# NSA attention in a two-layer decoder trunk: value products with the split values as weights, and the NSA norm moved behind the output projection

## The chip, the cores and the metric

One NeuronCore of a Trainium2 chip runs the whole program. The time is device microseconds (us) of one execution; the runs given below are separate executions of the same program. Engines: PE (TensorE, matrix products and transposes), DVE (VectorE), ACT (ScalarE), POOL (GpSimd), SP (SyncE, which issues most of the DMAs).

## The reference

Two layers, each of four parts on 512 tokens of 1024 features: a half-step FFN, a hybrid token mixer, cross-attention to 256 memory tokens, and another half-step FFN. The change is in the mixer:

```python
o_nsa = nsa_mixer(q_n, kc, vc, ks, vs, kw, vw, gates, ...)   # 8 heads of 64
o_nsa = rms_norm(o_nsa, nsa_out_g)                            # over its 512 features
o_ret = retention(q_r, k_r, v_r, g_r, ret_gn_g)               # 4 heads of 128
return jnp.concatenate([o_nsa, o_ret], axis=-1) @ w_out
```

`nsa_mixer` sums three branches for each head, weighted by gates: attention over 31 compressed blocks, over selected blocks and over a window. With 512 tokens the selected and the window branch both see every key up to the query, so both are plain causal attention with an ALiBi slope, with keys and values of their own. `retention` multiplies the scores by a decay instead of a softmax and normalises each head.

## The kernel before

Activations stand feature-major in eight [128 features x 512 tokens] chunks. Most products are made of two float32r parts for each operand (`unit` L82 and `split` L122 make a high part on ACT, whi or oh, and the rest on DVE, wlo or ol); `mm3` (L116) then issues three float32r matmuls (L117 to L119). Products with small or few operands are in plain fp32.

`mixer` (L398) runs once per layer. It computes the compressed branch (`cmp_attn`), then 16 head-branches, 8 heads by 2 branches. For one branch `head_scores` (L589) makes, for each of the four query blocks, two score matmuls (keys as high and low part, ps_s, 512, 384, 256 and 256 columns), a DVE operation that adds ALiBi and takes the extreme of the row (L610), and the exponential on ACT with its sum (L612). `head_out` (L615) makes ten transposes of p (ps_pt), copies them to SBUF (pT, ACT or DVE), ten fp32 products with the block of pT as the stationary and 64 columns of values as the moving operand (L634, ps_po), scales by gate over sum on DVE (L640) and adds to onsa [tokens x features] on POOL (L642). `head_out` of a branch is written behind `head_scores` of the next.

Then come the inputs of retention: qr and kr (`fm_plain`, ps_fm) and vr and gr (`tm`, token-major, ps_tm); the norm of onsa (L673 to L681); `ret_scores` (L693: ps_rs, times decay on DVE, ra); `to_fm` (L684), which transposes onsa and splits it (ps_ot, oh, ol); `ret_out` (L705: ps_ro, normalisation and gate on DVE, oret); `to_fm` for oret; `out_proj` (L215), eight output chunks of 24 matmuls each (ps_o); and `postnorm`.

The order on each engine is set when the program is built, by a scheduler that draws independent work forward; each engine then runs its list in order and waits where an operand is not there. PSUM has eight tiles of a bank: four for the accumulators of the projections (`acc`: ps_fm, ps_tm, ps_o) and four for the rest (`aux`: ps_s, ps_pt, ps_po, ps_rs, ps_ro, ps_ot). SBUF tiles come from pools with a fixed number of buffers. So ps_fm, ps_tm and ps_o matmuls stand as filler between the steps of the heads and of retention, as far as accumulators allow.

## Time and profile before

| | |
|---|---|
| median of 3 runs | 2512.14 us (2511.12 to 2512.42) |
| span of the profiled execution | 2510.8 us |
| PE busy | 2447.7 us, 97% |
| DVE busy | 1389.5 us, 55% |
| ACT busy | 902.0 us, 36% |
| POOL busy | 260.9 us, 10% |
| mixer of layer 0, first score of the first branch | 508.2 us |
| first score of the 16th branch | 625.8 us |
| end of the last ps_o matmul | 721.5 us |

The busy shares are means over the whole span; the windows of the mixer show them stage by stage. PE's matmuls are pipelined and a record's duration contains the drain, so the price of one matmul is read from the distance between starts. The granted clock (PEclk) is a share of full speed, 2.4 GHz; the lower level is 1.2 GHz.

### The profile page before, as it was taken

The page shows a single profiled execution, that of the slowest core. Times are in us where ns is not written, and L with a number is a line of the kernel's source. Part 1 is how long each engine was busy: PE and PEld are TensorE (multiplying, and loading weights), DVE is VectorE, ACT ScalarE, POOL GpSimd, SP SyncE. Part 2 cuts the span into 40 slices and gives each one's busy share as a digit, 9 for nine tenths or more (in the row PEclk, how much of TensorE's full clock was granted, in tenths as well). Part 3 has the DMA queues.
Part 4 walks back from the last instruction along what each step waited for, and adds up shares of the span by engine and source line. Part 5 has one row for each costly group of instructions (what it writes and reads, how often), then busy time and mean ns, then how long its engine had stood idle before and what let it go on. Part 6 is the DMA issues. An engine that isn't in the chain of part 4 may idle for free.

```text
span 2510.8 us, 31031 instructions
## 1 busy us (share of the span) xinstructions
PE 2447.7 (97%) x12184; PEld 2039.7 (81%) x12184; DVE 1389.5 (55%) x2518; ACT 902.0 (36%) x1480; POOL 260.9 (10%) x218
## 2 busy tenths in 40 slices
PE   8999999999999999999999999999999998999997
PEld 6888878888877878888878888878888777888887
DVE  6434458465776574344474344574657765634454
ACT  4322243255344442322342222332553543322222
POOL 0000023001040120000120000130010402100002
PEclk9999999999999999999999999999999999999999
DMA  4323343411232233233323232324112322232321
GB/s 170 100 98 95 98 121 109 145 43 35 76 109 85 93 101 95 98 93 100 111 101 96 97 93 101 109 93 144 43 34 70 101 68 67 86 100 92 102 94 58
DMA packets 74594, 233.64 MB, mean 93 GB/s; under 512 B 8272, under 2 KB 17744, under 8 KB 74448
## 3 DMA queue, kind: packets, MB, share of 16 engines
q1 hardware_dynamic: 65232, 222.21, 27.8%
q10 hardware_dynamic: 9216, 9.44, 1.3%
q8 instruction: 96, 1.57, 0.3%
q14 instruction: 50, 0.41, 0.1%
HBM read 229.53 MB, written 2.10 MB: 92 GB/s over the span
## 4 chain that ended last, share of the span: by engine, by line
PE 89%; DVE 7%; ACT 2%; DMA 1%; issue 1%; POOL 0%; SPq 0%; POOLq 0%; ACTq 0%; DVEq 0%
PE ps_gu L118 12%; PE ps_gu L117 12%; PE ps_gu L119 12%; PE ps_dn L118 6%; PE ps_dn L119 6%; PE ps_dn L117 6%; PE ps_po L634 3%; PE ps_o L118 2%; PE ps_o L119 2%; PE ps_o L117 2%; DVE xsl L184 2%; PE ps_fm L118 2%; PE ps_fm L119 2%; PE ps_fm L117 2%; PE ps_tm L118 1%; PE ps_tm L119 1%
## 5 line engine op out<-in xcount | busy, mean ns | idle before, releaser
L88 ACT ACTIVATE whi<-raw 128x1024 fp32r<-128x1024 f32 (+2 forms) x402 | 417.8, 1040 | 1104.2 <-PE ps_gu L118 331.5
L89 DVE TENSOR_TENSOR wlo<-raw,whi 128x1024 fp32r<-128x1024 f32 (+2 forms) x402 | 491.6, 1223 | 295.6 <-ACT whi L88 289.1
L117 PE MATMUL ps_gu<-xsh,whi 128*128 128x512 f32 (+1 forms) x1424 | 552.0, 389 | 11.9 <-ACT whi L88 9.0
L118 PE MATMUL ps_gu<-xsl,whi 128*128 128x512 f32 (+1 forms) x1424 | 554.8, 390 | 7.8 <-DVE xsl L184 7.4
L119 PE MATMUL ps_gu<-xsh,wlo 128*128 128x512 f32 (+1 forms) x1424 | 552.3, 388 | 0.8 <-DVE wlo L89 0.7
L118 PEld LDWEIGHTS ps_gu<-xsl,whi 128*128 128x128 f32 x1424 | 268.6, 189 | 70.0 <-DVE xsl L184 16.3
L117 PEld LDWEIGHTS ps_gu<-xsh,whi 128*128 128x128 f32 x1424 | 268.7, 189 | 66.4 <-ACT whi L88 9.0
L119 PEld LDWEIGHTS ps_gu<-xsh,wlo 128*128 128x128 f32 x1424 | 268.6, 189 | 55.4 <-DVE wlo L89 1.9
L157 POOL TENSOR_TENSOR ssq<-ssq,sq 128x512 f32<-128x512 f32 (+1 forms) x84 | 131.9, 1571 | 1714.3 <-ACT sq L156 1711.3
L118 PE MATMUL ps_dn<-hl,whi 128*128 128x512 f32 (+1 forms) x704 | 268.4, 381 | 2.2 <-DVE hl L126 2.2
L117 PE MATMUL ps_dn<-hh,whi 128*128 128x512 f32 (+1 forms) x704 | 268.2, 381 | 0.0
L119 PE MATMUL ps_dn<-hh,wlo 128*128 128x512 f32 (+1 forms) x704 | 268.0, 381 | 0.0
L278 DVE TENSOR_TENSOR u<-ps_gu,rstd_bc 128x512 f32<-128x512 f32 x88 | 60.8, 691 | 217.8 <-PE ps_gu L119 217.8
L274 DVE TENSOR_TENSOR g<-ps_gu,rstd_bc 128x512 f32<-128x512 f32 x88 | 60.8, 691 | 184.0 <-PE ps_gu L119 181.2
L118 PEld LDWEIGHTS ps_dn<-hl,whi 128*128 128x128 f32 x704 | 132.3, 188 | 28.9 <-DVE hl L126 3.4
L117 PEld LDWEIGHTS ps_dn<-hh,whi 128*128 128x128 f32 x704 | 132.3, 188 | 25.6
L119 PEld LDWEIGHTS ps_dn<-hh,wlo 128*128 128x128 f32 x704 | 132.3, 188 | 25.0
L301 DVE TENSOR_TENSOR y<-ps_dn,y 128x512 f32<-128x512 f32 x56 | 38.7, 691 | 131.6 <-PE ps_dn L119 131.6
L118 PE MATMUL ps_fm<-xsl,whi 128*128 128x512 f32 x256 | 104.6, 409 | 3.4 <-DVE xsl L184 3.3
L117 PE MATMUL ps_fm<-xsh,whi 128*128 128x512 f32 x256 | 103.3, 405 | 0.0
L119 PE MATMUL ps_fm<-xsh,wlo 128*128 128x512 f32 x256 | 102.2, 400 | 1.0 <-DVE wlo L89 1.0
L612 ACT ACTIVATE p<-p,smx 128x512 f32<-128x512 f32 (+3 forms) x128 | 70.4, 552 | 87.2 <-DVE smx L610 87.0
(226 smaller groups left out, 3749.7 us busy)
## 6 DMA issues: line engine op xcount, KB each, us to landing
raw<-in_ffn_gu_dram SPq DMA_DIRECT2D x176, 512.0 KB, 3.3
raw<-in_ffn_dn_dram SPq DMA_DIRECT2D x64, 448.0 KB, 3.3
raw<-in_ffn_dn_dram SPq DMA_DIRECT2D x32, 512.0 KB, 3.5
raw<-in_win_fm_dram SPq DMA_DIRECT2D x32, 512.0 KB, 3.3
raw<-in_wk_dram SPq DMA_DIRECT2D x16, 512.0 KB, 3.5
raw<-in_cmp_w_dram SPq DMA_DIRECT2D x16, 512.0 KB, 3.7
raw<-in_wout_dram SPq DMA_DIRECT2D x16, 512.0 KB, 3.5
raw<-in_wv_dram SPq DMA_DIRECT2D x16, 512.0 KB, 3.5
```

The costliest lines, as they stand in the source:

```text
L88: act.activation(hi, raw, AF.Copy)
L89: dve.tensor_tensor(lo, raw, hi.bitcast(F32), op=ALU.subtract)
L117: pe.matmul(ps, ah, bh, start=start, stop=False)
L118: pe.matmul(ps, ah, bl, start=False, stop=False)
L119: pe.matmul(ps, al, bh, start=False, stop=stop)
L157: eng.tensor_tensor(acc_t, acc_t, sq, op=ALU.add)
L184: dve.scalar_tensor_tensor(lo, x[c][:, ts_], g, hi.bitcast(F32), op0=ALU.mult, op1=ALU.subtract)
L274: dve.tensor_tensor(g1, pss[0], bc, op=ALU.mult)
L278: dve.tensor_tensor(u1, pss[1], bc, op=ALU.mult)
L301: dve.tensor_tensor(y[c], ps, y[c], op=ALU.add)
L612: act.activation(pr[i], pr[i], AF.Exp, bias=m, scale=-1.0, accum_out=sums[:, i : i + 1])
L634: pe.matmul(po[:, i], blk[i, j], vsel[j // 2][:, j % 2, col : col + DH], start=j == 0, stop=j == i)
```

## The change

The value products change sides: the values of a key block, split into high and low part side by side (vsel, 128 columns of weights), are the stationary operand, and the transposed probabilities, split too (pTh on ACT, pTl on DVE), move. For key block j all queries from block j on move at once: 512, 384, 256 and 128 columns, in float32r, each twice (high and low). Both branches of a head accumulate into one ps_po tile, whose lower and upper 64 rows are the products with the two parts of the values; ACT copies one half, DVE adds the other, POOL adds to onsa, which is now feature-major [128 x 512] in four chunks. Since the result is feature-major, the gate over the sum can't be applied to it per row; p itself is multiplied by it on DVE, before the transposes. The compressed branch is normalised ahead of its transposes too, and its products become feature-major.

The transposes of onsa fall away: each chunk is gained and split as it is. Its norm is a factor per token, and that is applied behind the projection: `out_mixed` computes the NSA half of an output chunk, multiplies it by the row nsa_bc (1/rms, broadcast by PE) and adds the retention half, accumulated in a bank of its own. The squares of onsa are summed on ACT, POOL and DVE. In `down_halves` the fourth chunk's weights are held in buffers of another pool.

```diff
...
             y.append(yc)
         return y, ssq
+    def out_mixed(src, l, parts, bc):
+        (h1, l1), (h2, l2) = parts
+        y, ssq = [], None
+        w = {}
+        def half(c, oh, ol, k0):
+            wh, wl = w[c]
+            ps = acc("ps_o")
+            for k in range(4):
+                s = slice((k0 + k) * P, (k0 + k + 1) * P)
+                mm3(ps, wh[:, s], wl[:, s], oh[k], ol[k], k == 0, k == 3)
+            return ps
+        def scaled(c):
+            t = big("yn")
+            ps = half(c, h1, l1, 0)
+            dve.tensor_tensor(t, ps, bc(), op=ALU.mult)
+            return t
+        def both(c, t):
+            nonlocal ssq
+            ps = half(c, h2, l2, 4)
+            yc = big("y")
+            dve.tensor_tensor(yc, ps, t, op=ALU.add)
+            ssq = sumsq(ssq, yc, c, dve if c == NC - 1 else pool)
+            y.append(yc)
+        for c in range(3):
+            w[c] = unit(src[l, c], 1024)
+        ts = [scaled(c) for c in range(3)]
+        for c in range(3):
+            both(c, ts[c])
+        for c in range(3, NC):
+            w[c] = unit(src[l, c], 1024)
+            both(c, scaled(c))
+        return y, ssq
     def out_halves(src, l, oh, ol, gains, nxt):
...
                 parts = []
                 for k0 in (0, 4):
                     m = min(4, n - k0) * P
-                    h_, l_ = big("dh", F32R, tag="xs")[:, :m], big("dl", F32R, tag="xs")[:, :m]
+                    tag = "kv" if c == 3 else "xs"
+                    h_, l_ = big("dh", F32R, tag=tag)[:, :m], big("dl", F32R, tag=tag)[:, :m]
                     act.activation(h_, raw[:, k0 * P : k0 * P + m], AF.Copy)
                     dve.tensor_tensor(l_, raw[:, k0 * P : k0 * P + m], h_.bitcast(F32), op=ALU.subtract)
                     parts += [(h_[:, k * P : (k + 1) * P], l_[:, k * P : (k + 1) * P]) for k in range(m // P)]
...
             if b == 0:
                 compressed(0, hid_k)
         hid_v = hidden(ph)
-        vsel = [big("vsel", shape=(P, 2, 256)) for _ in range(2)]
+        vsel = []
         gates = sp.tile([P, NT, 24], F32, name="gates", tag="gates", bufs=2)
         for i, ps in enumerate(tm(a["win_vg"][l], 280, 3)):
-            act.activation(vsel[i // 2][:, i % 2], ps[:, :256], AF.Copy, scale=cols[:, i : i + 1])
+            t = big("vsel", F32R, shape=(P, 4, 2, DH))
+            pv4 = ps[:, :256].rearrange("p (u d) -> p u d", u=4)
+            act.activation(t[:, :, 0], pv4, AF.Copy, scale=cols[:, i : i + 1])
+            dve.scalar_tensor_tensor(t[:, :, 1], pv4, cols[:, i : i + 1], t[:, :, 0].bitcast(F32), op0=ALU.mult, op1=ALU.subtract)
+            vsel.append(t)
             act.activation(gates[:, i], ps[:, 256:280], AF.Copy, scale=cols[:, i : i + 1])
         compressed(1, hid_v)
         act.activation(gates, gates, AF.Tanh, scale=0.5)
...
-        o_nsa = bp.tile([P, NT, T], F32, name="onsa", tag="onsa", bufs=1)
+        o_nsa = [bp.tile([P, T], F32, name="onsa", tag="onsa", bufs=4) for _ in range(4)]
         tcm = []
         for u in range(2):
...
             dve.reciprocal(r, sm_)
             r2 = tiny("crg", H)
             dve.tensor_tensor(r2, r, gates[:, i].rearrange("p (h b) -> p h b", b=3)[:, :, 0], op=ALU.mult)
-            pt = aux("ps_ct")
+            dve.tensor_tensor(s, s, r2.unsqueeze(2).to_broadcast([P, H, 32]), op=ALU.mult)
+            return pc
+        def cmp_out(pcs):
             for g in range(2):
-                pe.transpose(pt[:, g * P : (g + 1) * P], pc[:, g * P : (g + 1) * P], ident)
-            pT = big("cpT")[:, :256]
-            act.activation(pT, pt[:, :256], AF.Copy)
-            po = aux("ps_co")
-            for g in range(2):
-                pe.matmul(po[:, g * 256 : (g + 1) * 256], pT[:, g * P : (g + 1) * P], vb[:, g], start=True, stop=True)
-            dve.tensor_tensor(o_nsa[:, i].rearrange("p (h d) -> p h d", h=H), po.rearrange("p (h d) -> p h d", h=H),
-                              r2.unsqueeze(2).to_broadcast([P, H, DH]), op=ALU.mult)
+                pt = aux("ps_ct")
+                for i in range(NT):
+                    pe.transpose(pt[:, i * P : (i + 1) * P], pcs[i][:, g * P : (g + 1) * P], ident)
+                pT = big("cpT")
+                act.activation(pT, pt, AF.Copy)
+                for c in range(2):
+                    po = aux("ps_co")
+                    pe.matmul(po, vb[:, g, c * P : (c + 1) * P], pT, start=True, stop=True)
+                    act.activation(o_nsa[2 * g + c], po, AF.Copy)
         kst = {}
         def stack_keys(g):
...
                 dve.tensor_tensor_reduce(pr[i], ps[:, :n], alibi[:, T - n :], scale=-(2.0 ** -(h + 1)), scalar=3.0e38,
                                          op0=ALU.add, op1=ALU.min, accum_out=m)
                 act.activation(pr[i], pr[i], AF.Exp, bias=m, scale=-1.0, accum_out=sums[:, i : i + 1])
-            return pr, sums
-        def head_out(h, b, pr, sums):
-            g = h // 4
-            col = b * P + g * DH
...
             rc = tiny("src", NT)
             dve.reciprocal(rc, sums)
             rg = tiny("srg", NT)
             dve.tensor_tensor(rg, rc, gates[:, :, h * 3 + 1 + b], op=ALU.mult)
-            ob = big("ob")[:, :256].rearrange("p (i d) -> p i d", i=NT)
-            dve.tensor_tensor(ob, po, rg.unsqueeze(2).to_broadcast([P, NT, DH]), op=ALU.mult)
-            oi = o_nsa[:, :, h * DH : (h + 1) * DH]
-            pool.tensor_tensor(oi, oi, ob, op=ALU.add)
-        for i in range(NT):
-            cmp_attn(i)
+            for i in range(NT):
+                dve.tensor_scalar(pr[i], pr[i], rg[:, i : i + 1], None, op0=ALU.mult)
+            return pr
+        outs = {}
+        def head_out(h, b, pr):
+            g = h // 4
+            if b == 0:
+                outs[h] = aux("ps_po")
+            po = outs[h]
+            for grp in ((0,), (1, 3), (2,)):
+                pt = aux("ps_pt")
+                w = sum(NT - j for j in grp) * P
+                if w == T:
+                    hi, lo = big("pTh", F32R), big("pTl", F32R)
+                else:
+                    t = big("pThl", F32R)
+                    hi, lo = t[:, :w], t[:, w : 2 * w]
+                o, at = 0, {}
+                for j in grp:
+                    at[j] = o
+                    for i in range(j, NT):
+                        pe.transpose(pt[:, o : o + P], pr[i][:, j * P : (j + 1) * P], ident)
+                        o += P
+                act.activation(hi, pt[:, :w], AF.Copy)
+                dve.tensor_tensor(lo, pt[:, :w], hi.bitcast(F32), op=ALU.subtract)
+                for j in grp:
+                    v = vsel[j][:, 2 * b + g].rearrange("p s d -> p (s d)")
+                    n = (NT - j) * P
+                    for part in (hi, lo):
+                        pe.matmul(po[:, j * P :], v, part[:, at[j] : at[j] + n], start=b == 0 and j == 0 and part is hi,
+                                  stop=b == 1 and j == 2 and part is lo)
+            if b == 1:
+                own = slice((h % 2) * DH, (h % 2 + 1) * DH)
+                oth = slice((1 - h % 2) * DH, (2 - h % 2) * DH)
+                t = big("ob")
+                act.activation(t[own], po[oth], AF.Copy)
+                dve.tensor_tensor(t[own], po[own], t[own], op=ALU.add)
+                oi = o_nsa[h // 2][own]
+                pool.tensor_tensor(oi, oi, t[own], op=ALU.add)
+        cmp_out([cmp_attn(i) for i in range(NT)])
         prev = None
         for h in range(H):
             if h % 4 == 0:
                 stack_keys(h // 4)
             q2 = head_query(h)
             for b in range(2):
-                cur = (h, b) + head_scores(h, b, q2)
+                cur = (h, b, head_scores(h, b, q2))
                 if prev:
                     head_out(*prev)
                 prev = cur
         head_out(*prev)
+        def put(src, c, tag="h"):
+            return split(src, "o", sm[:, G_NSA + c : G_NSA + c + 1], tag=tag)
+        nsa = [put(o_nsa[c], c, "b") for c in range(4)]
+        ssq = None
+        for c in range(4):
+            ssq = sumsq(ssq, o_nsa[c], c, dve if c == 3 else pool)
+        nsa_bc = []
+        def nsa_row():
+            if not nsa_bc:
+                t = big("nsa_bc")
+                act.activation(t, row_bc(rms_cols(ssq, 512, T), NT), AF.Copy)
+                nsa_bc.append(t)
+            return nsa_bc[0]
         qr = [fm_plain(8 + h, "qr", "h") for h in range(RH)]
         kr = [fm_plain(12 + h, "kr", "h") for h in range(RH)]
         vr = []
...
             act.activation(t, ps, AF.Copy, scale=cols[:, i : i + 1])
             gr.append(t)
-        sq = tiny("nsq", NT)
-        for i in range(NT):
-            t = big("sq")
-            act.activation(t, o_nsa[:, i], AF.Square, accum_out=sq[:, i : i + 1])
-        v = tiny("nsv", NT)
-        dve.tensor_scalar(v, sq, 1.0 / 512, EPS, op0=ALU.mult, op1=ALU.add)
-        r = newton(v, NT)
-        for i in range(NT):
-            dve.tensor_scalar(o_nsa[:, i], o_nsa[:, i], r[:, i : i + 1], None, op0=ALU.mult)
-        oh, ol = [], []
         def to_fm(c, tiles):
             pt = aux("ps_ot")
             for i in range(NT):
                 pe.transpose(pt[:, i * P : (i + 1) * P], tiles[i], ident)
-            h_, l_ = split(pt, "o", sm[:, G_NSA + c : G_NSA + c + 1], tag="h")
-            oh.append(h_)
-            ol.append(l_)
+            return put(pt, c)
         def ret_scores(h):
             dec = big("dec")
             nc.scalar.dma_start(dec, a["decay"][h])
...
             th = big("th")
             act.activation(th, gr[i], AF.Tanh, scale=0.5)
             dve.scalar_tensor_tensor(gr[i], th, 1.0, gr[i], op0=ALU.add, op1=ALU.mult)
-        for c in range(4):
-            to_fm(c, [o_nsa[:, i, c * P : (c + 1) * P] for i in range(NT)])
         ons = [ret_out(h, ats[h]) for h in range(RH)]
-        for h in range(RH):
-            to_fm(4 + h, [ons[h][:, i] for i in range(NT)])
+        ret = [to_fm(4 + h, [ons[h][:, i] for i in range(NT)]) for h in range(RH)]
         if prep:
             prep()
-        y, ssq = out_proj(a["wout"], l, oh, ol)
+        y, ssq = out_mixed(a["wout"], l, [zip(*nsa), zip(*ret)], nsa_row)
         postnorm(y, ssq, gcols(l, G_MIXPOST), nxt)
     def xattn(l, nxt, filler=None, mid=None, prep=None, halves=False):
         kk, vv = {}, {}
```

How the change moves instructions is shown at three places, in layer 0. A row is the line, the operation, output<-inputs and the size of the output; x4 means four in a row. On PE, around the last two branches' value products (ps_po; ps_tm is filler), before:

```order
L634 MATMUL ps_po<-vsel,pT 128x64 x4
L625 MATMUL ps_pt<-cst,p 128x128 x6
L117 MATMUL ps_tm<-whi,xsh 128x512
L118 MATMUL ps_tm<-wlo,xsh 128x512
L119 MATMUL ps_tm<-whi,xsl 128x512
L117 MATMUL ps_tm<-whi,xsh 128x512
L118 MATMUL ps_tm<-wlo,xsh 128x512
L634 MATMUL ps_po<-vsel,pT 128x64 x6
L119 MATMUL ps_tm<-whi,xsl 128x512
L117 MATMUL ps_tm<-whi,xsh 128x512
```

and after, where also the first retention scores (ps_rs) stand between them:

```order
L698 MATMUL ps_po<-pThl,vsel 128x256 x2
L698 MATMUL ps_po<-pTh,vsel 128x512
L690 MATMUL ps_pt<-cst,p 128x128 x3
L698 MATMUL ps_po<-pTl,vsel 128x512
L690 MATMUL ps_pt<-cst,p 128x128 x3
L119 MATMUL ps_tm<-whi,xsl 128x512
L117 MATMUL ps_tm<-whi,xsh 128x512
L698 MATMUL ps_po<-pTh,vsel 128x384
L118 MATMUL ps_tm<-wlo,xsh 128x512
L119 MATMUL ps_tm<-whi,xsl 128x512
L768 MATMUL ps_rs<-qr,kr 128x512
L698 MATMUL ps_po<-pTl,vsel 128x384
```

Before, 67 ps_tm matmuls follow the last ps_po; after, the last ps_tm stands ahead of it.

On DVE, ahead of retention's first multiplies (ra; memg is memory work of the cross-attention), before:

```order
L681 TENSOR_SCALAR onsa<-onsa,rs_y 128x512 x4
L89 TENSOR_TENSOR wlo<-raw,whi 128x1024
L364 SCALAR_TENSOR_TENSOR memg<-memc,small_72,memg 128x256
L89 TENSOR_TENSOR wlo<-raw,whi 128x1024
L702 TENSOR_TENSOR ra<-ps_rs,dec 128x512
L702 TENSOR_TENSOR ra<-ps_rs,dec 128x384
L702 TENSOR_TENSOR ra<-ps_rs,dec 128x256
L702 TENSOR_TENSOR ra<-ps_rs,dec 128x128
```

and after:

```order
L89 TENSOR_TENSOR wlo<-raw,whi 128x1024
L705 TENSOR_TENSOR ob<-ps_po,ob 64x512
L129 SCALAR_TENSOR_TENSOR ol<-onsa,small_72,oh 128x512 x4
L157 TENSOR_TENSOR ssq<-ssq,sq 128x512
L769 TENSOR_TENSOR ra<-ps_rs,dec 128x512
L769 TENSOR_TENSOR ra<-ps_rs,dec 128x384
L769 TENSOR_TENSOR ra<-ps_rs,dec 128x256
L769 TENSOR_TENSOR ra<-ps_rs,dec 128x128
```

The last ob add, the four splits ol and the last add of the squares (ssq) have moved ahead of ra, the weight splits (wlo) in between are gone, and the norm's multiplies of onsa too.

On PE, from retention's outputs (ps_ro) to the projection, before:

```order
L687 MATMUL ps_ot<-cst,onsa 128x128 x16
L117 MATMUL ps_o<-oh,whi 128x512 x4
L709 MATMUL ps_ro<-vr,ra 128x128 x40
L687 MATMUL ps_ot<-cst,oret 128x128 x4
L118 MATMUL ps_o<-ol,whi 128x512
L119 MATMUL ps_o<-oh,wlo 128x512
L117 MATMUL ps_o<-oh,whi 128x512
```

and after, from the transposes of the last retention head on:

```order
L119 MATMUL ps_o<-oh,wlo 128x512
L756 MATMUL ps_ot<-cst,oret 128x128
L164 MATMUL rms_ps<-ones,ssq 128x64
L756 MATMUL ps_ot<-cst,oret 128x128
L164 MATMUL rms_ps<-ones,ssq 128x64
L756 MATMUL ps_ot<-cst,oret 128x128 x2
L164 MATMUL rms_ps<-ones,ssq 128x64 x2
L117 MATMUL ps_o<-oh,whi 128x512
L118 MATMUL ps_o<-ol,whi 128x512
L119 MATMUL ps_o<-oh,wlo 128x512
L173 MATMUL bc_ps<-cst,rs_y 128x128 x4
L117 MATMUL ps_o<-oh,whi 128x512
```

Before, ps_o goes on in a long row right behind ps_ro. After, three ps_o follow each head's transposes, and the long row, 144 matmuls, begins behind bc_ps, the broadcast of 1/rms.

## Rows read from the trace of the kernel before

**Rows 1.** The page: busy us, shares and instructions; below, the chain that ended last.

```profile
PE 2447.7 (97%) x12184; PEld 2039.7 (81%) x12184; DVE 1389.5 (55%) x2518; ACT 902.0 (36%) x1480; POOL 260.9 (10%) x218
...
PE 89%; DVE 7%; ACT 2%; DMA 1%; issue 1%; POOL 0%; SPq 0%; POOLq 0%; ACTq 0%; DVEq 0%
```

**Rows 2.** Windows of layer 0: length, busy us of PE, PEld, DVE, ACT, POOL; PEclk; DMA.

```profile
508.20:625.80 117.60, 116.73 (x742) 100.50 (x742) 65.15 (x202) 64.90 (x170) 13.05 (x13) 1.00 0.13 41
625.80:721.50 95.70, 94.68 (x505) 78.73 (x504) 63.50 (x200) 35.83 (x65) 14.09 (x9) 1.00 0.29 89
```

**Rows 3.** Timeline of PE: start, us, engine, line, operation, out<-in, count [idle before]; float32r scores.

```profile
508.49 0.39 PE L608 MATMUL ps_s<-kstl,q 128*128 128x512 f32 x1
508.72 0.34 PE L607 MATMUL ps_s<-ksth,q 128*128 128x384 f32 x1
508.89 0.35 PE L608 MATMUL ps_s<-kstl,q 128*128 128x384 f32 x1
509.08 0.28 PE L607 MATMUL ps_s<-ksth,q 128*128 128x256 f32 x1
509.19 0.28 PE L608 MATMUL ps_s<-kstl,q 128*128 128x256 f32 x1
```

**Rows 4.** Timeline of PE: fp32 matmuls, two records each.

```profile
624.28 1.06 PE L634 MATMUL ps_po<-vsel,pT 128*128 128x64 f32 x8
625.18 0.83 PE L625 MATMUL ps_pt<-cst,p 128*128 128x128 f32 x6
...
667.51 9.20 PE L709 MATMUL ps_ro<-vr,ra 128*128 128x128 f32 x80 [0.92 <-DVE ol L129]
```

**Rows 5.** Groups on DVE, 478 to 745 us: count | busy, mean ns | idle before.

```profile
L629 DVE COPY pT<-ps_pt 128x512 f32<-128x512 f32 x8 | 5.5, 686 | 0.0
...
L681 DVE TENSOR_SCALAR onsa<-onsa,rs_y 128x512 f32<-128x512 f32 x4 | 1.7, 482 | 0.1
```

**Rows 6.** Group on ACT, 505 to 745 us: the last exponential of a branch.

```profile
L612 ACT ACTIVATE p<-p,smx 128x128 f32<-128x128 f32 x16 | 6.2, 387 | 0.0
```

**Rows 7.** Groups on ACT (same window) and POOL (whole span); landing times of the decay tiles.

```profile
L128 ACT ACTIVATE oh<-ps_ot,small 128x512 fp32r<-128x512 f32 x8 | 5.2, 688 | 28.8 <-PE ps_ot L687 20.6 <-DVE oret L724 8.2
...
L157 POOL TENSOR_TENSOR ssq<-ssq,sq 128x512 f32<-128x512 f32 x65 | 117.0, 1800 | 1059.3 <-ACT sq L156 1056.6 <-issue 1.2
...
DMA to landing us min/median/max: 2.7/2.9/3.6
```

**Rows 8.** Timeline of DVE in the tail of layer 0.

```profile
655.81 1.73 DVE L702 TENSOR_TENSOR ra<-ps_rs,dec 128x512 f32<-128x512 f32 x4 [2.98 <-PE ps_rs L701]
657.46 1.22 DVE L89 TENSOR_TENSOR wlo<-raw,whi 128x1024 fp32r<-128x1024 f32 x1
...
666.71 2.72 DVE L129 SCALAR_TENSOR_TENSOR ol<-ps_ot,small,oh 128x512 fp32r<-128x512 f32 x4
670.04 0.89 DVE L714 BATCH_NORM_STATS2 bst<-ps_ro 128x6 f32<-128x128 f32 x4 [0.61 <-PE ps_ro L709]
...
682.92 0.75 DVE L129 SCALAR_TENSOR_TENSOR ol<-ps_ot,small,oh 128x512 fp32r<-128x512 f32 x1 [0.84 <-ACT oh L128]
...
689.23 0.17 DVE L144 SCALAR_TENSOR_TENSOR rs_y<-rs_u,rs_y 128x4 f32<-128x4 f32 x1
...
690.71 0.90 DVE L724 SCALAR_TENSOR_TENSOR oret<-oret,gr 128x128 f32<-128x128 f32 x4
...
692.77 0.75 DVE L129 SCALAR_TENSOR_TENSOR ol<-ps_ot,small,oh 128x512 fp32r<-128x512 f32 x1 [0.20 <-ACT oh L128]
```

**Rows 9.** Windows around an idle time of PE, then PE behind it.

```profile
748.00:752.00 4.00, 0.43 (x2) 0.00 (x0) 3.69 (x4) 1.06 (x1) 2.09 (x2) 1.00 0.43 135
752.00:756.00 4.00, 3.54 (x15) 2.98 (x16) 3.20 (x11) 0.00 (x0) 0.00 (x0) 0.69 0.00 0
...
753.74 0.63 PE L118 MATMUL ps_mv<-wlo,memg 128*128 128x512 f32 x1
754.16 0.63 PE L118 MATMUL ps_xq<-xsl,whi 128*128 128x512 f32 x1
```

More of the change, by code (lines that the diff above doesn't have):

```diff
@@ L309, in down_halves @@
         for c in range(NC):
-            if c < 4:
+            if c < 3:
                 wh, wl = unit(src[c][:, f0 * P : (f0 + n) * P], n * P)
@@ L612, in head_scores @@
                 act.activation(pr[i], pr[i], AF.Exp, bias=m, scale=-1.0, accum_out=sums[:, i : i + 1])
-            return pr, sums
-        def head_out(h, b, pr, sums):
-            g = h // 4
-            col = b * P + g * DH
-            po = aux("ps_po")[:, :256].rearrange("p (i d) -> p i d", i=NT)
-            for grp in ((3,), (2, 0), (1,)):
-                pt = aux("ps_pt")
-                pT = big("pT")
-                w, blk = 0, {}
-                for i in grp:
-                    for j in range(i + 1):
-                        pe.transpose(pt[:, w : w + P], pr[i][:, j * P : (j + 1) * P], ident)
-                        blk[i, j] = pT[:, w : w + P]
-                        w += P
-                if b == 0 and len(grp) == 1:
-                    dve.tensor_copy(pT[:, :w], pt[:, :w])
-                else:
-                    act.activation(pT[:, :w], pt[:, :w], AF.Copy)
-                for i in grp:
-                    for j in range(i + 1):
-                        pe.matmul(po[:, i], blk[i, j], vsel[j // 2][:, j % 2, col : col + DH], start=j == 0, stop=j == i)
             rc = tiny("src", NT)
```

## The prediction, made before the changed kernel ran

> **What bounds the kernel now.** I read the busy shares and the chain of waits first: PE is busy 97% of the span and makes up 89% of the chain [rows 1]. Then the windows of layer 0's mixer, cut at a mark that both kernels have, the last branch's first score matmul (625.8 us), and at the end of the last ps_o (721.5). From the first branch's first score (508.2) to the mark PE works 116.73 of 117.60 us, and from there to the end 94.68 of 95.70; DVE has 65.15 and 63.50 [rows 2]. So PE is the bound in both stretches, and a us of PE work there is a us of the kernel, until another engine's chain is longer. Layer 1 repeats the pattern; I work out layer 0 and double it.
>
> **Prices on PE** are distances between starts, since durations overlap. A float32r matmul takes .23 us at 512 columns (508.49 to 508.72), .17 at 384 and .11 at 256 [rows 3]. In plain fp32 a product is two records: 80 ps_ro records last 9.20 us, so .23 for one 128-column product, and eight ps_po records of 64 columns take .90, so .225 for one product [rows 4]: in fp32 the halved width saved nothing.
>
> **To the mark.** By the order of the two programs, between the first and the last branch's first score stand before 134 fp32 ps_po products, and after 28, 27, 26 and 26 float32r ones of 512, 384, 256 and 128 columns. Removed: 134 x .225 = 30.1. Added: 28 x .23 + 27 x .17 + 26 x .11 = 13.9, and the 26 narrow ones. No float32r matmul of this kernel has under 256 columns, so their price is open: below, .11, which is what 256 columns and any single record here cost; above, the .23 of an fp32 product of 128 columns. I take .23, the only row of that width for a product (6.0), and keep .11 (2.9) for the range. The Trainium skill, "TensorE: Matmul & The Clock Gate", section "Wait — 56ns, not 53.3ns?", gives start to start as the columns over 2.4 GHz plus about 2.5 ns, 56 ns at 128 columns. By it the narrow ones would be 1.5 us in all and the sum below 4.5 less; the rows at 256 columns agree with it, those at 512 lie a little above (it gives .216), and no row shows the width.
>
> Filler moves as well. Of the token-major projections (ps_tm) 170 matmuls stand ahead of the mark instead of 106: 64 x .23 = 14.7 us that lay behind it. (Three ps_fm pass the first score, which shifts both ends alike.) Transposes and scores are as many as before. Sum: -30.1 + 13.9 + 6.0 + 14.7 = **+4.5** (with .11: +1.4), so 122 us instead of 117.6.
>
> **Does DVE keep up there?** Per branch it gains four multiplies of p (128 to 512 columns; the row at 512 takes .48, so about 1.3 as an estimate) and three subtractions from PSUM (two of 512 at .69, one of 256 at about .4: 1.8), and half an ob add (.34). It loses the ob multiply (256 columns, .4) and on average half of a 512 and a 256 copy (.55) [rows 5]. That is +2.5 by durations, which overlap a little, say +2.1; x 15 = 32 on top of 65 [rows 2]: 97 of 122 us. New on DVE is a wait in its order: the reciprocal of the sums and the four multiplies stand behind the last exponential of the same branch (.39 on ACT [rows 6], after the wider ones and the reading of its sum). Queued behind that on DVE are the next pTl subtractions, for which PE's ps_po wait. At about 1 us per branch, an estimate from twice that row and its hand-overs, DVE needs 112 of 122. So PE's own work covers it; 0 in the sum, up to +2 per layer in the range.
>
> **From the mark to the end** it took 95.7 [rows 2]. PE's work falls: 64 ps_tm (14.7) are gone, 26 ps_po products (5.9) become 21 float32r ones (3.8), 16 transposes of onsa (1.8) go and 8 fp32 products of the norm (1.8) come: 94.7 becomes some 78. But the chain is another one now, since DVE's order puts the last square of onsa ahead of retention's multiplies ra. PE ends the last ps_po 12.7 us after the mark (22 ps_tm 5.1, 20 transposes 2.2, eight scores 1.2, ps_po 3.8, one ps_rs .4). Then ACT copies ob (.69), DVE adds (.69), POOL adds into onsa (1.80, by 512 columns), ACT splits chunk 3 (.69) and squares two chunks (1.4), POOL adds two (3.6), DVE adds the last (.69) [rows 5, 7]; with eight hand-overs of about .1 that is **23.0**. Queued behind that last add on DVE are ra and all of retention, for which PE waits. The decay tiles are issued on ACT's queue behind the squares and take 2.9 to land [rows 7], so they come no later than POOL's two adds.
>
> From there DVE sets the pace. ra and gr took from 655.81 to 666.71, with a weight split of 1.2 inside: 9.7. The four splits at 666.71 now stand ahead of ra, in POOL's shadow. The four heads' norms from 670.04 to 691.61, less a wait of .84, are 20.7, and the last transposes and splits to 693.52 are 1.9 [rows 8]. 23.0 + 9.7 + 20.7 + 1.9 = 55.3. What follows is new at this place: twelve small operations for 1/rms (.17 each, .2 from start to start: 2.4), bc_ps (four products, .9), ACT's copy nsa_bc (.69), the first yn from PSUM (.69), with hand-overs 60.2. Only that frees an accumulator: three of the four banks hold NSA halves that wait for nsa_bc, the fourth the first retention half, so only 48 of the 192 ps_o can run ahead. The other 144 x .23 = 33.1 follow: **93.3**, so **-2.4**. Between the end of ps_ro (ra ends at about 30, plus 9.2 for ps_ro) and 60 PE has some 6 us of work and idles for 15: that is where its saving goes.
>
> **The clock.** An idle of PE (.43 us busy of 4.00, from 748) was followed by a window with granted clock .69, in which 512-column matmuls stand .42 apart [rows 9]: the lower of the two levels, 1.2 GHz. 4 us at .69 lose 1.2 us of work, and the spell ran on a little. In the new gap PE does a short burst about every 5 us, so I expect the lower level there, 1.6 us lost once the 144 start, and .4 for bc_ps and the last transposes: **+2.0** (0 to 4). The same page of the Trainium skill, section "Part 1: The HAM clock gate (the "warmup" mystery)", calls the throttled clock the resting state, which activity lifts; the rows at 748 agree.
>
> **At nothing:** the compressed branch (the same PE work in wider matmuls); down_halves (other buffers for a weight chunk); cross-attention and the FFNs, whose order is the same.
>
> **Sum.** Per layer 4.5 - 2.4 + 2.0 = +4.1, twice +8.2: the profiled 2510.8 becomes 2519.0. The median of the runs lies 1.3 above that profile, so **about 2520 us**, 0.3% slower. 0.2% (5 us) is about what a measurement of this kernel can tell from no change.
>
> **Rivals.**
> - *PE stays the bound in the tail too* (faster). If POOL's and DVE's work there is shorter than I have it, or more of the projection runs ahead, the saving comes back whole: -30.1 + 13.9 + 2.9 (6.0) to the mark and -2.1 behind it, 12 to 15 per layer: 2481 to 2488. Against it: four banks only, and a chain of single operations that nearly all have rows. Half of it gives 2502. Chance .18.
> - *Cheap narrow matmuls and no clock loss* (no change): 1.4 - 2.4 = -1.0 per layer, 2510; with only one of the two, 2514 to 2516. For it: .11 is a price that rows show, for other kinds. Chance .28.
> - *DVE becomes the bound in the head stage* (slower still). It decides once the wait for the exponential exceeds (122 - 97) / 15 = 1.7 us per branch, for instance because ACT, which now makes all copies of the transposes, is two copies (.69 each [rows 7]) behind. At 2.2 it costs 15 x .5 = 7.5 per layer: 2535. Chance .14.
> - *The float32r products are no faster than fp32 ones*: at twice their price 13.9 more per layer, 2548. Against it: the same kind gives the scores their .11 to .23 [rows 3]. Chance .02.
>
> **How the numbers follow.** The forecast (2515 to 2525) has .38. Faster by over 0.2%: the first rival and the lower edge of the second, .20. Same: the rest of the second and the near edge of the forecast, .29. Slower: .51. The range goes down to halfway into the first rival (2495) and up to the DVE rival (2536).
>
> **What would show it.** Right: the mark 4 us later per layer, PE idle by 10 us or more between the last ps_ro and the long row of ps_o, a granted clock under 1.00 there, and narrow ps_po .2 apart. Wrong: PE without gaps up to the last ps_o (then the saving shows in the time), ps_o in numbers ahead of nsa_bc, or PE waiting for pTl in the head stage (then the DVE rival holds).

## The result

The changed kernel takes 2529.4 us (median of 4 runs, 2526.6 to 2531.1) against 2511.6 before: 1.0070 times as long, interval 1.0058 to 1.0082. The forecast was 2520 (2495 to 2536), slower, with 2515 to 2525 as its middle. Its span is 2529.2 us, against 2510.8. PE is as busy as before in sum, as its page's line of busy times shows beside that of [rows 1]:

```profile
PE 2445.9 (97%) x11784; PEld 2010.4 (79%) x11784; DVE 1473.5 (58%) x2713; ACT 931.1 (37%) x1527; POOL 254.3 (10%) x206
```

The windows at the same marks say where: length, busy us of PE, PEld, DVE, ACT and POOL, PEclk. First layer 0 and layer 1 up to the last branch's first score and from there to the last ps_o; then, in layer 0, the stretch from 664 to the long row, its part behind ps_ro, and the long row.

```profile
507.50:629.80 122.30, 121.58 (x648) 97.91 (x648) 103.89 (x293) 81.06 (x203) 7.73 (x6) 1.00 0.20 61
629.80:732.70 102.90, 91.60 (x409) 70.44 (x409) 66.50 (x201) 32.44 (x55) 15.99 (x10) 0.85 0.18 57
1773.90:1896.10 122.20, 121.46 (x647) 97.94 (x648) 103.80 (x293) 80.97 (x203) 7.74 (x6) 1.00 0.19 58
1896.10:1996.40 100.30, 89.05 (x409) 68.38 (x408) 66.47 (x201) 32.45 (x54) 16.24 (x10) 0.88 0.18 58
664.00:697.50 33.50, 24.18 (x122) 17.62 (x121) 27.76 (x137) 5.66 (x8) 0.00 (x0) 0.67 0.03 9
673.00:697.50 24.50, 15.47 (x44) 9.11 (x44) 19.56 (x94) 4.40 (x6) 0.00 (x0) 0.55 0.04 12
697.50:732.70 35.20, 35.18 (x145) 28.92 (x146) 16.71 (x20) 10.25 (x14) 10.40 (x6) 0.93 0.30 97
```

Against 117.60 and 95.70 [rows 2] the head stage is 4.7 longer in layer 0 and 4.6 in layer 1, the tail 7.2 and 4.6. (The first score comes .7 earlier per layer.) In the head stage PE still works all the time; in the tail it idles for 11 us of 102.9 and 100.3, and from 673.00 to the long row its granted clock is .55, so nearly always the lower of the two levels, 1.2 GHz. One of the four runs of e10 below took 3035 us at a mean granted clock of .75 and is left out of its numbers.

Ends of the steps of the tail, in us behind the mark, from the timelines; forecast without its 2.0 for the clock (the mark is 629.8 and 1896.1):

| | forecast | layer 0 | layer 1 |
|---|---|---|---|
| last ps_po | 12.7 | 14.0 | 14.0 |
| sum of squares on DVE | 23.0 | 23.3 | 23.5 |
| ra and gr | 32.7 | 36.9 | 35.1 |
| last head's oret | 53.4 | 59.2 | 57.4 |
| long row of ps_o begins | 60.2 | 67.7 | 65.9 |
| last ps_o | 93.3 | 102.9 | 100.3 |

The timeline of DVE in layer 0 (as in [rows 8]: start, us, line, operation, out<-in, count, idle before and its releaser) shows the two links that are late:

```profile
645.98 3.85 DVE L129 SCALAR_TENSOR_TENSOR ol<-onsa,small,oh 128x512 fp32r<-128x512 f32 x4
652.37 0.69 DVE L157 TENSOR_TENSOR ssq<-ssq,sq 128x512 f32<-128x512 f32 x1 [2.54 <-POOL ssq L157]
653.09 1.68 DVE L769 TENSOR_TENSOR ra<-ps_rs,dec 128x512 f32<-128x512 f32 x4
657.49 1.73 DVE L769 TENSOR_TENSOR ra<-ps_rs,dec 128x512 f32<-128x512 f32 x4 [2.72 <-PE ps_rs L768]
660.35 1.73 DVE L769 TENSOR_TENSOR ra<-ps_rs,dec 128x512 f32<-128x512 f32 x4 [1.12 <-PE ps_rs L768]
662.51 1.73 DVE L769 TENSOR_TENSOR ra<-ps_rs,dec 128x512 f32<-128x512 f32 x4 [0.43 <-PE ps_rs L768]
664.16 2.57 DVE L798 SCALAR_TENSOR_TENSOR gr<-th,gr 128x512 f32<-128x512 f32 x4
666.64 0.88 DVE L781 BATCH_NORM_STATS2 bst<-ps_ro 128x6 f32<-128x128 f32 x4
...
688.11 0.89 DVE L791 SCALAR_TENSOR_TENSOR oret<-oret,gr 128x128 f32<-128x128 f32 x4
691.05 0.16 DVE L166 TENSOR_SCALAR rms_v<-rms_ps 128x4 f32<-128x4 f32 x1 [2.05 <-PE rms_ps L164]
```

DVE waits 2.54 for POOL, as forecast, then 2.72, 1.12 and .43 for ps_rs, which the forecast did not have. On PE the reason stands ahead of those ps_rs (in the first row PE waits for the first of the four splits ol, which ends at 647.84):

```profile
647.90 0.69 PE L118 MATMUL ps_o<-ol,whi 128*128 128x512 f32 x1 [1.33 <-DVE ol L129]
...
650.52 0.63 PE L117 MATMUL ps_o<-oh,whi 128*128 128x512 f32 x1
650.95 0.63 PE L118 MATMUL ps_o<-ol,whi 128*128 128x512 f32 x1
...
656.21 0.39 PE L119 MATMUL ps_o<-oh,wlo 128*128 128x512 f32 x1
656.44 2.32 PE L768 MATMUL ps_rs<-qr,kr 128*128 128x512 f32 x8
...
688.54 0.44 PE L756 MATMUL ps_ot<-cst,oret 128*128 128x128 f32 x1 [1.14 <-DVE oret L791]
...
697.52 0.79 PE L117 MATMUL ps_o<-oh,whi 128*128 128x512 f32 x1 [1.41 <-DVE yn L247]
...
698.53 0.63 PE L119 MATMUL ps_o<-oh,wlo 128*128 128x512 f32 x1
698.96 0.63 PE L117 MATMUL ps_o<-oh,whi 128*128 128x512 f32 x1
```

PE's order has 30 ps_o between the first and the second head's ps_rs. They begin at 647.90 and then run without a gap until 656.44, so it is their 8.5 us of work that delays those ps_rs, and not a wait for the last ol (649.83), as the expectations of e3 and e12 below have it. In layer 0 the first eight of them also ran at the lower level, .43 apart; layer 1 has no such spell (see the last section). The long row begins at 697.52, behind nsa_bc, and its first matmuls are .43 apart.

### The profile page after: what moved, and what is told of

Same layout as the page of the kernel before. It is cut to its first block, busy times and chain, and to the rows that moved or that the text cites. A ratio compares the mean times of both kernels' runs of the same rounds, so it can differ in the third digit from the quotient of the medians.

```text
span 2529.2 us, 30461 instructions
## 1 busy us (share of the span) xinstructions
PE 2445.9 (97%) x11784; PEld 2010.4 (79%) x11784; DVE 1473.5 (58%) x2713; ACT 931.1 (37%) x1527; POOL 254.3 (10%) x206
## 5 line engine op out<-in xcount | busy, mean ns | idle before, releaser
L212 POOL TENSOR_TENSOR x<-x,yn 128x512 f32<-128x512 f32 (+1 forms) x56 | 80.1, 1464 | 92.6 <-DVE yn L211 92.6
```

Of the source, the lines that this page charges most:

```text
L212: (dve if c == 0 else pool).tensor_tensor(x[c][:, ts_], x[c][:, ts_], t, op=ALU.add)
```

## The experiments

Four theories. A: the swap of the value products is a gain for PE, which is lost because retention and the NSA norm set the end of the tail while the projection can't run ahead. B: the lower clock. C: the head stage, through DVE. And the forecast's own link, POOL's adds ahead of ra.

**The two parts apart.** e4 keeps the new value products and puts the norm back in front of the projection, with its row made behind `ret_scores`:

```diff
-        nsa = [put(o_nsa[c], c, "b") for c in range(4)]
...
+        row = nsa_row()
+        for c in range(4):
+            dve.tensor_tensor(o_nsa[c], o_nsa[c], row, op=ALU.mult)
+        nsa = [put(o_nsa[c], c) for c in range(4)]
         ons = [ret_out(h, ats[h]) for h in range(RH)]
...
-        y, ssq = out_mixed(a["wout"], l, [zip(*nsa), zip(*ret)], nsa_row)
+        y, ssq = out_proj(a["wout"], l, [h_ for h_, _ in nsa + ret], [l_ for _, l_ in nsa + ret])
```

> The first part of the change alone: value products with the split values as weights, feature-major output, but the norm stands in front of the projection as before (the row 1/rms is made behind retention's scores, DVE multiplies the four chunks by it, then they are split) and the projection is the old one. Theory A (the swap of the value products is a gain of some 11 us of PE per layer, and the norm behind the projection is what loses it): 61 ps_o or so can run between the retention heads as before, no gap, the tail 80 to 88 us, 2487 to 2502. Theory C (the swap itself costs, through DVE): 2515 or more.

Measured: 2515.8, 1.0017 (1.0007 to 1.0026). So the norm's place makes most of the loss, but the swap alone is no gain either, against A as stated. The tail is 93.2 us long, not 80 to 88: of the ps_tm that had stood there as filler 22 are left instead of 86, the others having run in the head stage, and PE now waits ahead of ps_ro. PE's waits in e4's tail (line, releaser: us in total, times, longest):

```profile
PE ps_rs L767 <- DVE ra L768: 5.4, 1, 5.4
PE bc_ps L173 <- DVE rs_y L144: 4.3, 1, 4.3
```

e5 is the other part alone, the norm behind the projection on the old value products. Against the kernel before, with the row made where the projection asks for it:

```diff
-        r = newton(v, NT)
-        for i in range(NT):
-            dve.tensor_scalar(o_nsa[:, i], o_nsa[:, i], r[:, i : i + 1], None, op0=ALU.mult)
...
-        y, ssq = out_proj(a["wout"], l, oh, ol)
+        y, ssq = out_mixed(a["wout"], l, [(oh[:4], ol[:4]), (oh[4:], ol[4:])], nsa_row)
```

> The second part of the change alone: the kernel before with its fp32 value products and token-major output, but without the multiplies of onsa by 1/rms; the row 1/rms is made and broadcast late, and the projection is the changed one (NSA halves times the row, retention halves added). Theory A (the late row holds the banks): the head stage stays at 117.6 us, behind the last retention head come about 2.4 for 1/rms, .9 for bc_ps, 1.4 for the copy and the first multiply, and then 144 ps_o (32.7) instead of 130 in a row from there: the tail from the mark grows from 95.7 to 104 to 107, so 2512 + 2 x (8 to 11) = 2528 to 2534, more than the whole change loses. If the loss of the change comes from its value products instead: 2512 to 2516.

Measured: 2533.4, 1.0083 (1.0068 to 1.0098). Head stage 117.5, tail 105.4 and 105.6 (forecast of A: 104 to 107). That part alone loses 20.7 us, more than both parts together.

**Closing the gap.** e2 makes the row right behind `ret_scores` and loads the weights in halves, the eight NSA halves first and the retention halves after them, so that all eight scaled halves can be ready before retention's (they lie in the buffers of tag xs):

```diff
         ats = [ret_scores(h) for h in range(RH)]
+        nsa_row()
...
-        for c in range(3):
-            w[c] = unit(src[l, c], 1024)
-        ts = [scaled(c) for c in range(3)]
...
+        for c in range(NC):
+            w[c] = unit(src[l, c][:, :512], 512)
+            ts.append(scaled(c))
+        for c in range(NC):
+            w[c] = unit(src[l, c][:, 512:], 512)
             both(c, ts[c])
```

> The changed kernel with two edits: 1/rms of the NSA output and its broadcast are made right behind retention's scores instead of behind its last head, and the weights of the projection are loaded and split in halves (512 columns each), so that all eight NSA halves can run ahead of retention's outputs and give their banks back. Theory A (PE's saving goes into the gap because banks wait for the row): the gap closes, 60 ps_o instead of 144 stand behind the last transposes, the tail from the last branch's first score to the last ps_o falls from 103 to 80 to 86, 2529 - 2 x (15 to 21) = 2487 to 2499. Theory C (the loss lies in the head stage or in DVE's own load, which this adds to): little comes back, 2520 or more.

e3 does all of e2 and moves one block more, so that put, squares and row all stand behind `ret_scores`:

```diff
-        nsa = [put(o_nsa[c], c, "b") for c in range(4)]
-        ssq = None
...
         ats = [ret_scores(h) for h in range(RH)]
+        nsa = [put(o_nsa[c], c, "b") for c in range(4)]
+        ssq = None
...
+        nsa_row()
```

> As e2, and the splits and squares of the NSA output are written behind retention's scores, so that on DVE ra no longer waits for POOL's sum of squares and on PE the ps_rs of the second head no longer stand behind 30 ps_o that wait for the last ol. Theory A with the late ps_rs as a part of its own (the trace of the changed kernel shows DVE waiting 4.3 us for ps_rs and 2.5 for POOL): another 2 to 6 us per layer where DVE's chain still ends the tail, 0 where PE does by then. PE's own work in the tail is some 78 us, which bounds it: not under 2484. Theory C: as e2, no gain.

Measured: e2 2505.9, .9979 (.9970 to .9989); e3 2495.1, .9937 (.9922 to .9952), faster than both kernels. e3's windows:

```profile
506.00:627.20 121.20, 120.22 (x642) 97.01 (x643) 102.95 (x295) 80.00 (x203) 7.74 (x6) 1.00 0.17 51
627.20:709.20 82.00, 79.74 (x415) 64.92 (x414) 65.22 (x209) 34.54 (x61) 12.11 (x9) 1.00 0.23 71
```

The tail of 82.0 has PE at work for 79.7, near the 78 of its own work; all waits of PE named in the two stages together are under 3.5 us. e2 came out above its range: its tail is 88.2. The row's first products (rms_ps) stand behind the late ps_rs and begin 34.2 behind the mark, PE then stands at bc_ps for 2.9 behind the small operations on DVE, and ps_ro, which follow bc_ps on PE, begin at 40.0 instead of 33.8. In e3, where the ps_rs come first, rms_ps begin at 29.2 and ps_ro at 34.1, and the time falls by a further 10.8 us (2 to 6 per layer expected). That is what this order is worth; e3 moves scores, splits and squares at once and doesn't part them.

e6 and e7 take e3's edits singly: e6 has the one added line `nsa_row()` of e2, e7 has the moved block of e3 without that line, so that the row still comes late.

> The changed kernel with one line more: 1/rms of the NSA output and its broadcast are made right behind retention's scores. The projection's order and weights are as in the change, so PE's list still has three ps_o behind each retention head and 147 in a row at the end. Theory A1 (the late row alone is the loss): the chain behind the last head is shorter by the 1/rms, bc_ps and the copy, 5 us per layer, 2518 to 2521. Theory A2 (the order of the weights and of the halves is what keeps filler away, and the row in front of ps_ro makes PE wait for DVE there, as in e2, where ps_ro began at 40 instead of 33): 2525 to 2531.

> The changed kernel with one block moved: splits, squares and sum of the NSA output are written behind retention's scores. The row stays late. In PE's list all 16 ps_rs stand ahead of the ps_o then, and on DVE ra ahead of the sum of squares. If the wait of ra for POOL's sum and of ps_rs for the last ol is on the chain as its trace says (ra begins 23 us after the mark, the last ends at 33 to 35): the last retention head ends 6 to 10 us earlier, PE's long row with it, 2529 - 2 x (6 to 10) = 2509 to 2517. If that only shifts the wait to the NSA splits, which DVE must do anyway before the row: 2523 to 2530.

Measured: e6 2525.6 (1.0050, 1.0035 to 1.0065), e7 2524.0 (1.0047, 1.0030 to 1.0064). Each is worth some 5 us (3.8 and 5.4 by the medians), hardly beyond the noise, since both intervals overlap that of the changed kernel, 1.0058 to 1.0082. The halves of the weights on top of e6's early row are worth 19.7 (e2 against e6); without the early row they were not tried. In e7 ra begins at 16.8 instead of 23.3, but the last oret ends at 54.6 instead of 57.4 to 59.2, because the NSA splits and squares now stand among retention's work on DVE, and the row still comes at the end. So neither of these two links holds the gap by itself: the row has to be early and the order of the weights has to let the projection use it. In e6 bc_ps ends 36.5 behind the mark and still 150 ps_o are left at 58.1, so banks that wait for the row are only a part; whether the rest is the written order of the halves or the buffers of the weights was not parted, since e2 changes both.

**What the swap is worth.** e9 puts e2's projection into the kernel before and keeps its old value products. Against the kernel before:

```diff
-        r = newton(v, NT)
-        for i in range(NT):
-            dve.tensor_scalar(o_nsa[:, i], o_nsa[:, i], r[:, i : i + 1], None, op0=ALU.mult)
...
+        nsa_row()
...
-        y, ssq = out_proj(a["wout"], l, oh, ol)
+        y, ssq = out_mixed(a["wout"], l, [(oh[:4], ol[:4]), (oh[4:], ol[4:])], nsa_row)
```

> The kernel before with the norm behind the projection as in e2: old fp32 value products, the row 1/rms made ahead of retention's scores, the projection's weights in halves and all NSA halves free to run ahead. It tells what the swapped value products are worth once the projection no longer makes PE wait (against e2 and e3). PE has no idle time to lose in this arrangement, as before, and a few fp32 products more for the row: 2511 to 2518. Then the swap is worth 6 to 12 us in the arrangement of e2 and some 16 to 22 in that of e3. If the swap is worth nothing, this one comes out at e3's 2495 or e2's 2506.

Measured: 2516.4, 1.0021 (1.0011 to 1.0030), in its range. Against e2 the new value products gain 10.5 us, against e3 21.3 (the latter with another order too). So A holds in this form: the swap gains, once the projection can run ahead.

**The clock.** e1, e8 and e10 add products by a tile of zeros to the sums of the first retention half, so that PE works in the gap: 12 ahead of each head's products (e1), or 16, 14, 14 and 20 (e8) and 10, 8, 8 and 8 (e10) behind them. e10's edit:

```diff
...
+                if c == 0 and k0 == 4:
+                    n = (10, 8, 8, 8)[k]
+                    for z in range(n):
+                        pe.matmul(ps, zero, h1[0], start=False, stop=k == 3 and z == n - 1)
```

> The changed kernel with 48 products by a tile of zeros added to the first retention half of the projection (12 ahead of each head's three ps_o, accumulated into the same bank, adding zero), so that PE works in the gap behind ps_ro. Nothing else moves. Theory A (the gap's cause is the chain of retention on DVE and the late 1/rms; the clock is a by-product): the gap stays, the granted clock in it is 1.00, and only the price of the spell comes back, about 12 matmuls at .43 instead of .227 after the gap (2.5 us) and the transposes, rms_ps and bc_ps in it (1 to 2 us): 3 to 5 us per layer, 2520 to 2524. Theory B (the lower clock is what costs): most of the loss against the kernel before comes back, 8 us or more per layer, 2513 or less. If the clock costs nothing: 2529.

> As e1, but the products by zeros stand only where PE is idle: 16, 14, 14 and 20 of them behind the three ps_o of each retention head, none ahead of ps_rs, and the last ones up to 1/rms and the start of the long row. In e1 the clock stayed at its upper level until the zeros ended, the stretch from the last head to the row got 1.8 us shorter, and the zeros ahead of ps_rs took that back. Expected here: upper level through the gap; 1.8 us per layer from the transposes and bc_ps, and up to 2.5 from the first matmuls of the long row if the upper level lasts until there; the 16 zeros of 3.6 us behind the last head may reach into the long row by up to 3. 2520 to 2527. If the clock were the main loss: 2515 or less.

> As e8 with fewer products by zeros (10, 8, 8 and 8 behind the three ps_o of each head), so that none reaches into the next transposes or into the long row. e8 had the upper level nearly throughout, but its zeros pushed the last head back by 2 to 3 us and filled 3.4 us of the long row. If the lower clock in the gap and behind it costs what e8's stretches say (1.6 us between the last head and the row, some 2.5 to 3 in the long row): 2529 - 2 x (3 to 5) = 2519 to 2523. If the clock costs nothing: 2529.

Measured: 2531.4 (1.0079, 1.0062 to 1.0095), 2527.5 (1.0060, 1.0045 to 1.0075) and 2527.5 (1.0066, 1.0049 to 1.0083). None gains what was expected. e10's windows of the stretch from 664 to the long row, and of the long row:

```profile
664.00:695.00 31.00, 25.88 (x134) 20.00 (x132) 24.59 (x131) 4.41 (x6) 0.00 (x0) 0.89 0.00 1
695.00:728.40 33.40, 32.81 (x145) 27.17 (x146) 17.28 (x21) 10.16 (x14) 10.52 (x6) 1.00 0.33 110
```

The long row of 144 takes 32.8 there instead of 35.2 and 34.4, and from the last oret (61.8 behind the mark) to its begin at 695.59, 68.4 behind it, 6.6 pass instead of 8.5. So by this comparison stretches at the lower level held 4.3 us in layer 0 and 3.5 in layer 1. But the zeros pushed the last oret back to 61.8 and 58.8 (59.2 and 57.4 without them), since retention's transposes queue behind them, and the times of e8 and e10 are only 1 to 2 us shorter, which is inside the noise. What the clock costs on balance stays open between nothing and the 7.8 of the stretches; that it is the main cause (B) was not shown.

**POOL and the narrow products.** e12 has all three adds on DVE:

```diff
-            ssq = sumsq(ssq, o_nsa[c], c, dve if c == 3 else pool)
+            ssq = sumsq(ssq, o_nsa[c], c, dve)
```

> The changed kernel with the three adds of the NSA squares all on DVE instead of two on POOL and one on DVE; the order of everything else is the same on each engine. The forecast had POOL's two adds (3.6 us) on the chain ahead of ra. In the changed kernel's trace they take 3.1, DVE waits 2.5 for them, and then DVE waits again, 2.7 and more, for the second head's ps_rs, which stand on PE behind 30 ps_o that wait for the last ol, not for the squares. Forecast's chain: the three adds on DVE (2.0) end some 2 us earlier and all of retention with them, 2524 to 2527. Theory A with the late ps_rs as the link that ends last: the wait moves from POOL to ps_rs, 2528 to 2530.

Measured: 2529.0, 1.0075 (1.0058 to 1.0093). DVE's timeline:

```profile
647.99 2.29 DVE L157 TENSOR_TENSOR ssq<-ssq,sq 128x512 f32<-128x512 f32 x3
650.31 1.68 DVE L769 TENSOR_TENSOR ra<-ps_rs,dec 128x512 f32<-128x512 f32 x4
653.85 1.73 DVE L769 TENSOR_TENSOR ra<-ps_rs,dec 128x512 f32<-128x512 f32 x4 [1.86 <-PE ps_rs L768]
656.70 1.73 DVE L769 TENSOR_TENSOR ra<-ps_rs,dec 128x512 f32<-128x512 f32 x4 [1.12 <-PE ps_rs L768]
...
660.51 2.57 DVE L798 SCALAR_TENSOR_TENSOR gr<-th,gr 128x512 f32<-128x512 f32 x4
```

The row of three adds ends at 650.28: the sum is done 22.2 us behind the mark instead of 23.3 (layer 1: 22.6 instead of 23.5), so the adds on DVE win 1 us and not 2. DVE waits for ps_rs instead. In layer 1 gr ends at 35.1 with and without the edit: there POOL was not on the chain. In layer 0 it ends at 35.0 instead of 36.9, but this execution has no spell at the lower level there, as the changed kernel's has (last section), and the time is the same.

e11 issues the 128-column products twice, so a block of the output is counted double:

```diff
-                    for part in (hi, lo):
+                    for part in (hi, lo, hi, lo) if j == 3 else (hi, lo):
```

> The changed kernel with the 128-column value products issued twice (the high and the low part of the last key block once more, so that block counts double in the output): 32 more narrow matmuls per layer, 30 of them ahead of the last branch's first score, where PE is busy 121.6 of 122.3 us. Price as forecast (.23): that mark 6.9 us later against the first score. Price as the changed kernel's trace has it (.06 to .09 from start to start): 1.8 to 2.7 later. By a full weight load of .11 each: 3.4.

Measured: the mark comes 125.7 us behind the first score in layer 0 and 123.6 in layer 1, 3.4 and 1.4 later. Summed from start to start in layer 0, 52 narrow ones take 5.1 us instead of 26 taking 2.3: .11 for each one added. (Past the mark fell 1 of the 170 ps_tm in layer 0, and 10 of them in layer 1, some 2.5 us, which explains its smaller shift.) Four products with the same weights in a row show it:

```profile
516.51 0.22 PE L698 MATMUL ps_po<-pTh,vsel 128*128 128x128 f32 x1
516.57 0.27 PE L698 MATMUL ps_po<-pTl,vsel 128*128 128x128 f32 x1
516.68 0.28 PE L698 MATMUL ps_po<-pTh,vsel 128*128 128x128 f32 x1
516.79 0.27 PE L698 MATMUL ps_po<-pTl,vsel 128*128 128x128 f32 x1
```

The second starts .06 behind the first, behind a wide product, and the others .11 apart, though none changes the weights.

## Why the prediction was right, and where it was not

- **Bound and place: right.** PE stayed the bound up to the mark, DVE did not become it (97.9 of 122.3 us, forecast 97 of 122), and of the 11 us that PE idles in the tail 9 lie between ps_ro and the long row (15.47 busy of 24.50 from 673.00 to 697.50), where the forecast had 15 and its own sign was 10 or more.
- **The mark: +4.7 and +4.6, forecast +4.5, by errors that cancel, so by luck in the size.** The narrow products were taken at .23 and cost .09 on the mean; the sign "narrow ps_po .2 apart" was wrong. These rows show value products of three key blocks (384, 128 and 256 columns) in a row:

```profile
568.07 0.33 PE L698 MATMUL ps_po<-pTl,vsel 128*128 128x384 f32 x1
568.24 0.22 PE L698 MATMUL ps_po<-pTh,vsel 128*128 128x128 f32 x1
568.30 0.27 PE L698 MATMUL ps_po<-pTl,vsel 128*128 128x128 f32 x1
568.50 0.39 PE L698 MATMUL ps_po<-pThl,vsel 128*128 128x256 f32 x1
568.72 0.39 PE L119 MATMUL ps_tm<-whi,xsl 128*128 128x512 f32 x1
```

  The second narrow one starts .06 behind the first, which agrees with the 56 ns of the Trainium skill ("TensorE: Matmul & The Clock Gate", "Wait — 56ns, not 53.3ns?"), measured there on bf16 products. The next starts are .20 and .22 later, for 128 and 256 columns, so that price doesn't hold for a whole series (e11: .11). So the narrow ones were 2.3 us instead of 6.0, but the wider ones 16.6 instead of 13.9: the 256-column ones cost .16 on the mean, not the .11 of [rows 3], and the 512-column ones .26. All of ps_po together took 18.9, forecast 19.9. The filler, 64 ps_tm, took 15.7 instead of 14.7.
- **The tail: the term that was mis-sized.** -2.4 for the work and +2.0 for the clock were forecast; +7.2 and +4.6 were measured. By the table the chain is late by these links. ra and gr end 13.6 and 11.6 behind the squares, taken at 9.7 from [rows 8]: that row doesn't hold the 30 ps_o that PE's new order puts ahead of ps_rs (8.5 us in layer 0). Retention's norms take 22.3, not 20.7; DVE's waits for ps_ro (.47 and .27 at 668 to 670) make .7 of it. From the last oret to the row 8.5, not 6.8, and the row 35.2 and 34.4, not 33.1: the clock, put at .4 and 1.6, held 1.9 and 2.4 (layer 1: 1.9 and 1.6) by e10's stretches.
- **POOL's adds as the link: wrong** (e12). The end of the squares was right to .5 us, but in layer 1, with the sum .9 earlier, gr ends no sooner, since ra still waits for ps_rs.
- **Why the saving didn't come back: right, and shown.** Where the projection can run ahead (e2, e3) the saving appears, in e3 with 2495 between the half and the whole of the first rival. e5 shows that the late norm loses 10 us per layer by itself. The forecast named the banks alone; e6 shows that an early row without the new order of the weights brings back only some 5 us.
- **The other rivals.** DVE set no pace in the head stage (C), and the float32r products were not at fp32's price. The sum, 8.2 forecast and 18.4 between the two spans, stayed in the range because that was drawn up to the DVE rival, which did not happen: that it held the time was luck, and the chain of retention, not a mechanism named as a rival, took the difference.

## What to carry to other kernels

A norm moved behind a product doesn't leave the path: the accumulators hold their banks until its row is there, so make the row as early as its inputs allow, and let every half that needs it run ahead. When work is taken from the bound engine, look at which chain the filler was hiding: here the scheduler pulled 64 matmuls forward into the head stage and left none behind the last value product. For every wait that a change adds, read the other engine's list up to the instruction that releases it.

## Not expected of the hardware

- A float32r product of 128 columns started .06 us behind one that followed a wide product, but in a series .11 apart even with the same weights (e11), where an fp32 product of 128 or 64 columns costs .23 [rows 4].
- A spell at the lower level also fell into the start of the NSA halves in layer 0 (ps_o .43 apart from 648 to 651) and not in layer 1, in the same execution of the same order; the tails differ by 2.6 us there. The two layers part at POOL's last add into onsa, which runs beside DVE's splits ol:

```profile
646.03 1.27 POOL L707 TENSOR_TENSOR onsa<-onsa,ob 64x512 f32<-64x512 f32 x1 [11.11 <-DVE ob L705]
1912.42 1.85 POOL L707 TENSOR_TENSOR onsa<-onsa,ob 64x512 f32<-64x512 f32 x1 [11.08 <-DVE ob L705]
```

  In layer 0 the add takes 1.27 and the first split beside it 1.86, so PE stands 1.33 before its first ps_o<-ol, and the spell follows. In layer 1 the add takes 1.85, the first split .75 and the second 1.78, PE stands only .22 and .50, and the clock stays up. A split with no add beside it takes .74. e10's layer 0 has the same wait and the same spell, but e6's layer 1 has the wait (1.31) without the spell, so the wait alone doesn't decide.
